# Mixers and projections of a hybrid diffusion step put into the kernel's own list schedule

## The chip, the cores and the metric

The kernel runs on one core of a Trainium2 chip. The metric is the device time of one launch in microseconds (us); the median of three runs of the kernel before is 824.52 us (822.47 to 827.32). Engines are called as the profile calls them: PE (TensorE, matmul) with PEld (its weight loads), DVE (VectorE), ACT (ScalarE), POOL (GpSimd) and SP (SyncE, which issues most DMAs).

## The reference, cut to what matters

One layer over 128 context and 512 latent tokens, model width 1024, everything in float32:

```python
h = rmsnorm(x, norm1_g) * (1 + scale1) + shift1
proj = h @ w_in                      # 1024 -> 3360 columns, split among four head groups
o_a = hgrn2_mixer(...)               # A: gated linear recurrence, two directions, 4 heads of 64
o_b = gla_mixer(...)                 # B: gated linear attention, two directions, 4 heads of 32
o_c = rglru_mixer(...)               # C: convolution, gates, elementwise recurrence (RG-LRU)
o_d = short_conv_mixer(...)          # D: short gated convolution
x = x + gate1 * (concatenate([o_a, o_b, o_c, o_d]) @ w_out)
h2 = rmsnorm(x, norm2_g) * (1 + scale2) + shift2
x = x + gate2 * (square(relu(h2 @ mlp_w1)) @ mlp_w2)
y = rmsnorm(x, final_norm_g)         # and the final states of A, B and C for the context
```

The scales, shifts and gates come from two condition vectors through a 1024 x 6144 matrix (`ada_w`).

## The kernel before

All 640 tokens stay on chip, channels on the partitions. Exact products are made of two rounded parts: a weight chunk is loaded raw (`rawX`), its rounded copy is `hiX`, the rest `loX` (`prep`, line 464), and each projection is 48 matmuls of 320 columns (hi x hi, hi x lo, lo x hi over eight blocks of the 1024 rows).

Four stages follow one another. In the start (0 to some 58 us) x is normalised and transposed, the first modulations are made, and the first chunks `a0` and `q` are projected by an order written out by hand (`START`). In the mixers (58 to 325 us) the names of `PLAN` (line 33) are gone through: a projection of one 128-channel half of a chunk (`cx0`), three units for each v projection (`vi0`), one modulation unit (`ada31`), or the next step of a job. There are four jobs, written as Python generators: `A0`, `A1` and `B` are `gla_job` (line 877), `RG` is `rg_job` (line 1083). A GLA job computes its lower-triangular products by doubling block sizes (`LEVELS`, 1 to 128): at each level a copy `K` of the keys (128 x 640), copies `Qb` of the queries (two 64 x 640 for A, eight 32 x 320 for B, whose heads are half as wide), small matmuls `sA` or `sB`, a masked copy of their results into `W`, and two DVE updates of `G` (lines 944, 945), which holds keys and queries and which the next level reads. Then come transposes `kt`, state sums `ds`, outputs `o`, and a norm over each head (`head_norms`, `NA` and `NB`). B takes over buffers of A0 and A1: there are two `G` and two `F` tiles. Projections share two PSUM buffers (`psA`, tag `mm`), weight chunks two hi/lo pairs and one raw buffer (`wpool`). Temporaries come from pools with a fixed number of buffers for each tag.

The order of instructions in the mixers is made by the framework's scheduler, which follows program order where operands are ready. Which engine makes a copy is looked up by name: `cp` (line 458) takes DVE if the name stands in `ON_DVE` (line 42), otherwise ACT. All copies of one level of one job have one name. `lnexp` (line 452) forces one ACT table set for a pair of functions.

From the output projection on (325 to 818 us), operations are not issued at once but recorded by a list planner (`Plan`, from line 146). Its engines record each call with a duration by formula (`cost`), the operations it depends on, and for tiles the regions read and written. `emit` computes for each operation the latest start that delays nothing after it, then goes through time: of the ready operations of the engine that comes free first, the one with the earliest latest start is issued. A DMA is priced at its bytes over one serial link plus 2 us. Tiles (`LateTile`) are placed when their first use is issued; tiles of one tag take their buffers in the order in which they were recorded (`Slots`). The MLP's matmuls keep their recorded order (`plan.chain`). Between mixers and MLP stand the gate row's store to DRAM (`gate_rows`, line 558), the split of the mixers' results (`put_o`, line 869) and the load and split of the output weights (`wo_v`, `wo_x`); before the change these were issued directly, and the pools of the MLP are opened when those of the mixers are closed.

## Time and profile before

| | |
|---|---|
| median of three runs | 824.52 us |
| profiled execution, time / span | 819.71 us / 817.9 us |
| busy PE / DVE / ACT / POOL | 778.8 / 575.2 / 420.3 / 23.4 us |
| busy PE in 58 to 325 us (mixers) | 255.0 of 267 us |
| busy DVE, ACT in 58 to 325 us | 201.3, 155.0 us |
| busy PE in 550 to 800 us (MLP) | 250.0 of 250 us |
| granted clock of PE | 1.00 in every slice to 800 us |

Busy is the union of the times in which an engine has an instruction in work. A matmul's shown time includes its passage through the array, so consecutive matmuls overlap, and PE can be busy throughout while its matmuls start later than they could. A chain of waits follows the end of a stretch back to what released each instruction.

### The profile page before, as it was taken

To read this page: it belongs to the slowest core of one execution; us is meant where nothing else is said; L and a number is where in the kernel's file an instruction comes from. 1 tells how busy PE (TensorE), PEld (TensorE's weight loads), DVE (VectorE), ACT (ScalarE), POOL (GpSimd) and SP (SyncE) were. 2 spreads that over 40 slices of the span, in tenths; PEclk is the share of its full clock that TensorE was granted. 3 is DMA by queue.
4 is the path that set the end of the run, shared out by engine and by line. 5 is a ranking of instruction groups with operands and counts; after the bars stand their busy time and mean duration, and the time that the engine had idled before them with its cause. 6 is when DMAs were issued, how large, how long until landed. Compare 5 with 4: busy or idle time off the path is not lost.

```text
span 817.9 us, 13749 instructions
## 1 busy us (share of the span) xinstructions
PE 778.8 (95%) x5536; PEld 682.7 (83%) x5536; DVE 575.2 (70%) x1061; ACT 420.3 (51%) x708; POOL 23.4 (3%) x48
## 2 busy tenths in 40 slices
PE   4999999999999989999899999899999999999995
PEld 3798988768777889888888989789899898998984
DVE  4779988857786376368997888647466475675757
ACT  7533549688486332156784706417246172371533
POOL 0040000101010000000000000000000000000001
PEclk9999999999999999999999999999999999999998
DMA  9723323333321522543653636513132041330313
GB/s 352 304 83 137 105 95 142 116 110 100 125 84 56 104 103 65 194 155 127 204 165 102 195 97 204 119 40 117 50 131 75 20 136 52 101 106 2 128 52 128
DMA packets 33696, 97.79 MB, mean 120 GB/s; under 512 B 8672, under 2 KB 9696, under 8 KB 29024
## 3 DMA queue, kind: packets, MB, share of 16 engines
q1 hardware_dynamic: 32544, 95.72, 35.5%
q10 hardware_dynamic: 576, 1.00, 0.4%
q8 instruction: 43, 0.70, 0.3%
q0 software_dynamic: 512, 0.20, 0.1%
q14 instruction: 21, 0.17, 0.1%
HBM read 91.44 MB, written 5.46 MB: 118 GB/s over the span
## 4 chain that ended last, share of the span: by engine, by line
PE 63%; DVE 15%; ACT 10%; DMA 8%; issue 3%; SPq 0%; DVEq 0%; ACTq 0%
PE ps L248 45%; DMA wq<-in_w_dram 4%; ACT QbB L462 2%; DVE xl L248 2%; PE pjcx L492 2%; PE pjdb L492 2%; PE pja L666 2%; DMA w2raw<-in_wout_dram 1%; PE ap L536 1%; DVE wq L248 1%; DMA w2raw<-in_w_dram 1%; PE pjbqk L492 1%; DVE big L248 1%; PE rg L1132 1%; DMA rawdb<-in_win_dram 1%
## 5 line engine op out<-in xcount | busy, mean ns | idle before, releaser
L248 PE MATMUL ps<-vh,olo 128*128 128x512 f32 x680 | 186.4, 390 | 1.0 <-DVE olo L248 0.7
L248 PEld LDWEIGHTS ps<-vh,olo 128*128 128x128 f32 x680 | 126.9, 188 | 28.8 <-DVE olo L248 1.9
L248 PE MATMUL ps<-vl,olo 128*128 128x512 f32 x320 | 99.3, 390 | 0.0
L248 ACT ACTIVATE vh<-w2raw 128x1024 fp32r<-128x1024 f32 x32 | 33.8, 1057 | 118.6 <-PE ps L248 114.2
L248 ACT ACTIVATE xh<-wq 128x512 fp32r<-128x512 f32 x96 | 59.4, 628 | 61.1 <-PE ps L248 43.9
L248 PE MATMUL ps<-yh,xh 128*128 128x320 f32 x256 | 79.5, 311 | 1.2 <-DVE rb L248 1.2
L248 PE MATMUL ps<-yl,xh 128*128 128x320 f32 x256 | 79.0, 309 | 0.0
L248 PE MATMUL ps<-yh,xl 128*128 128x320 f32 x256 | 79.0, 308 | 0.0
L248 DVE TENSOR_TENSOR h<-ps,h 128x512 f32<-128x512 f32 x60 | 38.6, 686 | 52.9 <-PE ps L248 52.6
L248 PEld LDWEIGHTS ps<-vl,olo 128*128 128x128 f32 x320 | 60.1, 188 | 12.7
L248 DVE TENSOR_TENSOR xl<-wq,xh 128x512 fp32r<-128x512 f32 x96 | 64.8, 687 | 8.1 <-ACT xh L248 7.9
L248 PE MATMUL ps<-ohi,xh 128*128 128x320 f32 x256 | 57.1, 310 | 0.5 <-ACT xh L248 0.4
L248 ACT ACTIVATE rb<-rb 128x640 f32<-128x640 f32 x64 | 46.8, 734 | 7.6 <-DVE rb L248 6.8
L248 PEld LDWEIGHTS ps<-yh,xh 128*128 128x128 f32 x256 | 48.1, 188 | 2.0 <-DVE rb L248 1.5
L248 PEld LDWEIGHTS ps<-yl,xh 128*128 128x128 f32 x256 | 48.1, 188 | 0.3
L248 PEld LDWEIGHTS ps<-yh,xl 128*128 128x128 f32 x256 | 48.1, 188 | 0.0
L248 DVE TENSOR_TENSOR vl<-w2raw,vh 128x1024 fp32r<-128x1024 f32 x32 | 39.0, 1220 | 8.1 <-ACT vh L248 7.4
L248 PEld LDWEIGHTS ps<-ohi,xh 128*128 128x128 f32 x256 | 42.8, 188 | 1.1 <-ACT xh L248 0.6
L248 PE MATMUL ps<-ohi,xl 128*128 128x320 f32 x128 | 39.8, 311 | 0.5 <-DVE xl L248 0.4
L248 DVE TENSOR_TENSOR olo<-rb,olo 128x640 fp32r<-128x640 f32 x32 | 26.3, 821 | 18.6 <-ACT olo L248 18.6
L248 PE MATMUL ps<-t,xh 128*128 128x320 f32 x128 | 28.7, 311 | 0.7 <-DVE rb L248 0.7
L248 ACT ACTIVATE rb<-ps 128x320 f32<-128x320 f32 x64 | 27.1, 424 | 4.1 <-PE ps L248 4.1
(426 smaller groups left out, 1677.7 us busy)
## 6 DMA issues: line engine op xcount, KB each, us to landing
ar<-in_ada_w_dram SPq DMA_DIRECT2D x20, 1024.0 KB, 4.9
wq<-in_w_dram SPq DMA_DIRECT2D x72, 256.0 KB, 3.7
w2raw<-in_w_dram SPq DMA_DIRECT2D x32, 512.0 KB, 4.4
big<-in_ada_g_dram SPq DMA_DIRECT2D x8, 512.0 KB, 3.5
x<-in_x_dram SPq DMA_DIRECT2D x5, 512.0 KB, 6.8
big<-in_x_dram SPq DMA_DIRECT2D x5, 512.0 KB, 4.2
x1d<-big SPq DMA_DIRECT2D x5, 512.0 KB, 2.6
xa<-x1d SPq DMA_DIRECT2D x5, 512.0 KB, 4.5
```

The source lines that it names most:

```text
L248: return fn(*[r(x) for x in a], **{w: r(v) for w, v in k.items()})
L462: act.activation(out, src, AF.Copy)
L492: pe.matmul(ps[:, n, :320], wt[:, k, c0:c0 + 128], h[:, k, s], start=(k == 0 and wt is hi and h is hhi), stop=stop)
L536: pe.matmul(ps[32 * g:32 * g + 32, :256], scx[:, 4 * j + g, 2 - 2 * vi:34 - 2 * vi], r3[:, 4 * j + g, :], start=(vi == 0 and j == 0), stop ...
L666: pe.matmul(d, w[:, k, 128 * j:128 * j + 128], (hlo if hi_ else hhi)[:, k, c], start=begin, stop=end, skip_group_check=(ch == "q" and i == 1))
L1132: pe.matmul(ps, wrg[:, dl, j, g, :], xc[:, hN * n:hN * n + hN], start=True, stop=True)
```

## The change

The mixers, their projections, the head norms, the split of the results and the output weights' loads are recorded by the same planner as the MLP, in one plan. `either` records a copy for two engines (`flex`): it is ready on both, and the one that takes it first keeps it. The plan is given times at which engines come free (`free`) and at which the first projections land (`ready`), counted from the mixers' start. Pools of the MLP open by events in the plan, after all uses of the pools whose place they take have been issued. A tile's later uses are ordered behind its first, and the latest start of a tile's first use is at most that of the next tile of the same tag. `PLAN` and the buffer counts stay; it now sets the recorded order, and with it the order in which tiles take their buffers.

```diff
--- before.py
+++ after.py
@@ -40,9 +40,7 @@
...
@@ -147,7 +145,8 @@
 
-    def __init__(self, nc, like):
+    def __init__(self, nc, like, ready=(), free=None):
+        self.ready, self.free, self.first, self.flex = dict(ready), dict(free or {}), {}, {}
         self.nc, self.like, self.ops, self.seen, self.masks = nc, like, [], {}, {}
         self.chain, self.last_pe, self.hint, self.tiles_of = False, None, None, {}
@@ -247,7 +246,22 @@
             r = lambda x: x.real() if isinstance(x, Late) else x
             return fn(*[r(x) for x in a], **{w: r(v) for w, v in k.items()})
+        for x in ins:
+            if not isinstance(x, Late):
+                for name, t in self.ready.items():
+                    if x.tensor.name.startswith(name):
+                        self.first[len(self.ops)] = t
         return self.add(eng, dur, go, ins, outs, mb, sets)
+
+    def either(self, act, dve, a):
+
+        i = self.record("DVE", dve, "tensor_copy", a, {})
+        other = self.ops[i][:3]
+        out, src = a
+        self.ops[i][:3] = ["ACT", self.cost("ACT", "activation", out, [src], (out, src, None), {})[0],
+                           lambda: act(*[x.real() if isinstance(x, Late) else x for x in a], AF.Copy)]
+        self.flex[i] = other
+        return i
     def add(self, eng, dur, fn, ins=(), outs=(), mb=0.0, sets=None, after=()):
         i = len(self.ops)
@@ -272,6 +286,8 @@
                     k.slots.queue.append(k)
                     if k.pool.opened is not None:
                         order.add(k.pool.opened)
+                elif k.users[0] != i:
+                    order.add(k.users[0])
                 k.users.append(i)
                 k.pool.users.append(i)
         if eng == "PE":
@@ -301,8 +317,15 @@
             for p, q in zip(x.queue, x.queue[x.n:]):
                 if max(p.users) < q.users[0]:
                     back.setdefault(q.users[0], []).extend(p.users)
+        before = {}
+        for x in slots:
+            for p, q in zip(x.queue, x.queue[1:]):
+                before.setdefault(q.users[0], []).append(p.users[0])
         for i in range(n - 1, -1, -1):
             eng, dur, _, deps, order, mb, _ = ops[i]
+            for d in before.get(i, ()):
+                if d < i:
+                    latest[d] = min(latest[d], latest[i])
             for d in deps:
                 e2, d2 = ops[d][0], ops[d][1]
                 latest[d] = min(latest[d], latest[i] - d2 - tail[d] - (hop[e2] if e2 != eng else 0.0))
@@ -317,7 +340,7 @@
                 after[d].append((i, True))
             for d in o[4]:
                 after[d].append((i, False))
-        at, free, ready, end_of = [0.0] * n, {}, {}, [0.0] * n
+        at, free, ready, end_of = [self.first.get(i, 0.0) for i in range(n)], dict(self.free), {}, [0.0] * n
         starts = {}
         for x in slots:
             for k in x.queue:
@@ -341,6 +364,8 @@
                         at[i] = max(at[i], end_of[j] + (0.03 if same else hop[ops[j][0]]))
                 x.taken += 1
             ready.setdefault(ops[i][0], []).append(i)
+            if i in self.flex:
+                ready.setdefault(self.flex[i][0], []).append(i)
         for i in range(n):
             if not left[i]:
@@ -362,6 +387,10 @@
             else:
                 i = min(xs, key=lambda x: (latest[x], x))
             ready[eng].remove(i)
+            if i in self.flex:
+                ready["ACT" if eng == "DVE" else "DVE"].remove(i)
+                if eng == "DVE":
+                    ops[i][:3] = self.flex[i]
             _, dur, _, deps, _, mb, sets = ops[i]
             load = None
             if sets and held not in sets:
@@ -448,15 +477,18 @@
         dve.reciprocal(rs, sd)
         return rs
+    recording = []
+
     @contextmanager
     def lnexp(after):
-        with tc.issue_after(after.ins):
-            ld = act.preload_act_table_set("natural_log_exp_and_others")
-        with tc.issue_after(ld.ins):
-            yield
+        plan.hint = "natural_log_exp_and_others"
+        yield
+        plan.hint = None
     def cp(name, out, src):
-        if name in ON_DVE:
+        if recording:
+            plan.either(real_nc.scalar.activation, real_nc.vector.tensor_copy, (out, src))
+        elif name in ON_DVE:
             dve.tensor_copy(out, src)
         else:
             act.activation(out, src, AF.Copy)
@@ -707,8 +739,14 @@
         dve.tensor_scalar(oml, lbt, -1.0, 1.0, op0=OP.mult, op1=OP.add)
     me_, ml_ = ExitStack(), ExitStack()
-    me = me_.enter_context(tc.tile_pool(name="mixe", bufs=1, reuse_waits="tile"))
-    mp = ml_.enter_context(tc.tile_pool(name="mixl", bufs=1, side="right", reuse_waits="tile"))
+    plan = Plan(nc, par[:, 0:1].tensor, ready={"pja0": 7.5, "pjq": 18.4}, free={"PE": 18.2, "ACT": 7.5, "DVE": 8.4})
+    me = LatePool(plan, me_.enter_context(tc.tile_pool(name="mixe", bufs=1, reuse_waits="tile")))
+    mp = LatePool(plan, ml_.enter_context(tc.tile_pool(name="mixl", bufs=1, side="right", reuse_waits="tile")))
+    real_nc, const0 = nc, const
+    recording.append(plan)
+    act, dve, pe, pool = plan.engines()
+    nc = Queues(plan, nc)
+    const, wpool, psA = LatePool(plan, const0), LatePool(plan, wpool, bufs=2), LatePool(plan, psA, psum=True, bufs=2)
     def tmp(nm):
         return mp.tile([128, 658], F32, name=nm, tag="tmp", bufs=NTMP)
@@ -717,6 +755,8 @@
         return tmp(nm)[:, :T]
     def sub(t, g, off, ap):
+        if isinstance(t, Late):
+            return t.view(lambda x: sub(x, g, off, ap))
         v = t[:, g, off:off + 1]
         return bass.AP(tensor=v.tensor, offset=v.offset, ap=[list(v.ap[0])] + ap)
@@ -1219,15 +1259,28 @@
         else:
             do_unit(u)
         if u == "q1":
-            psS_stack.close()
-            psB = stB.enter_context(tc.tile_pool(name="psB", bufs=2, space=PS, reuse_waits="tile"))
+            def open_psB():
+                psS_stack.close()
+                psB.real = stB.enter_context(tc.tile_pool(name="psB", bufs=2, space=PS, reuse_waits="tile"))
+
+            psB = LatePool(plan, psum=True, bufs=2)
+            psB.opened = plan.event(open_psB, range(len(plan.ops)))
     grow1 = gate_rows("gt1", nc.sync)
+    on_rows = on_first = list(range(len(plan.ops)))
     for j in jobs.values():
         assert next(j, None) is None
-    me_.close()
-    lp = ctx.enter_context(tc.tile_pool(name="mlp", bufs=1, reuse_waits="tile"))
+    lp, rp, ls, psN = (LatePool(plan) for _ in range(4))
+
+    def open_lp():
+        me_.close()
+        lp.real = ctx.enter_context(tc.tile_pool(name="mlp", bufs=1, reuse_waits="tile"))
+
+    lp.opened = plan.event(open_lp, me.users)
     oT["hi"] = [lp.tile([128, 2, T], F32R, name=f"ohi{i}", tag=f"ohi{i}") for i in range(4)]
     oT["lo"] = [lp.tile([128, T], F32R, name=f"olo{i}", tag=f"olo{i}") for i in range(8)]
+    VH, VL = ([lp.tile([128, D], F32R, name=f"{nm}{i}", tag=f"{nm}{i}") for i in range(4)] for nm in ("vh", "vl"))
+    BIG = [lp.tile([128, D], F32, name=f"big{i}", tag=f"big{i}") for i in range(2)]
+    WRAW2 = [lp.tile([128, D], F32, name=f"w2raw{i}", tag=f"w2raw{i}") for i in range(2)]
     for j in range(2):
         put_o(4 + j, [(slice(0, 128), hs[j][:, 0:128]), (slice(128, T), hs[j][:, 134:646])])
     for j in range(2):
@@ -1236,19 +1289,21 @@
         put_o(2 + j, [(ALL, pb[j]["o"])])
     for j in range(2):
         put_o(6 + j, [(ALL, dd["o", j])])
-    ml_.close()
-    hw_.close()
-    plan = Plan(nc, par[:, 0:1].tensor)
-    rp = LatePool(plan, ctx.enter_context(tc.tile_pool(name="mlpr", bufs=1, side="right", reuse_waits="tile")))
-    ls = LatePool(plan, ctx.enter_context(tc.tile_pool(name="mlps", bufs=1, reuse_waits="tile")))
-    stB.close()
-    psA_.close()
-    psN = LatePool(plan, ctx.enter_context(tc.tile_pool(name="psN", bufs=1, space=PS, reuse_waits="tile")), psum=True)
-    lp = LatePool(plan, lp)
-    VH, VL = ([lp.tile([128, D], F32R, name=f"{nm}{i}", tag=f"{nm}{i}") for i in range(4)] for nm in ("vh", "vl"))
-    BIG = [lp.tile([128, D], F32, name=f"big{i}", tag=f"big{i}") for i in range(2)]
-    WRAW2 = [lp.tile([128, D], F32, name=f"w2raw{i}", tag=f"w2raw{i}") for i in range(2)]
-    act, dve, pe, pool, sync = (Now(e) for e in (act, dve, pe, pool, nc.sync))
+
+    def open_rest():
+        ml_.close()
+        hw_.close()
+        rp.real = ctx.enter_context(tc.tile_pool(name="mlpr", bufs=1, side="right", reuse_waits="tile"))
+        ls.real = ctx.enter_context(tc.tile_pool(name="mlps", bufs=1, reuse_waits="tile"))
+
+    def open_psum():
+        stB.close()
+        psA_.close()
+        psN.real = ctx.enter_context(tc.tile_pool(name="psN", bufs=1, space=PS, reuse_waits="tile"))
+
+    rp.opened = ls.opened = plan.event(open_rest, [lp.opened] + wpool.users + mp.users + on_rows)
+    psN.psum = True
+    psN.opened = plan.event(open_psum, psA.users + psB.users + on_first)
     HT = T // 2
     HALVES = (slice(0, 512), slice(512, 1024))
...
...
```

## Rows read from the trace of the kernel before

**Rows 1.** The page, busy us (share of the span) xinstructions.

```profile
PE 778.8 (95%) x5536; PEld 682.7 (83%) x5536; DVE 575.2 (70%) x1061; ACT 420.3 (51%) x708; POOL 23.4 (3%) x48
```

**Rows 2.** Sums by stretch: length, busy PE, PEld, DVE, ACT, POOL, clock, DMA, GB/s.

```profile
58.00:325.00 267.00, 255.01 (x2588) 218.50 (x2587) 201.29 (x388) 154.98 (x248) 10.95 (x22) 1.00 0.31 101
58.00:110.00 52.00, 50.96 (x665) 48.23 (x664) 50.68 (x106) 20.41 (x29) 0.00 (x0) 1.00 0.30 106
200.00:270.00 70.00, 63.58 (x625) 52.25 (x626) 50.19 (x104) 46.54 (x85) 2.57 (x6) 1.00 0.24 80
270.00:325.00 55.00, 52.23 (x350) 49.70 (x351) 32.16 (x46) 15.45 (x21) 0.22 (x4) 1.00 0.33 84
325.00:550.00 225.00, 219.23 (x1149) 190.81 (x1149) 168.12 (x335) 114.09 (x204) 0.00 (x0) 1.00 0.47 146
550.00:800.00 250.00, 250.00 (x1398) 227.51 (x1397) 157.13 (x237) 112.50 (x187) 0.00 (x0) 1.00 0.26 83
```

**Rows 3.** Groups of PE's instructions, 58 to 325 us: count, busy us, mean ns, idle before.

```profile
L492 PE MATMUL pjcx<-hhi,hicx 128*128 128x320 f32 x32 | 7.4, 312 | 0.0
L536 PE MATMUL ap<-ar,scx 128*32 128x256 f32 x192 | 13.6, 383 | 0.5 <-ACT o2a L1073 0.5
L962 PE MATMUL sB<-QbB,KB 128*32 128x128 f32 x280 | 12.4, 277 | 3.6 <-ACT QbB L462 3.1 <-DVE QbB L460 0.5
L962 PE MATMUL sA<-QbA,KA 128*32 128x64 f32 x560 | 10.5, 221 | 0.8 <-DVE QbA L460 0.8
L1132 PE MATMUL rg<-xc,wrg 128*128 128x323 f32 x32 | 12.0, 471 | 0.7 <-ACT gr L1143 0.6
```

**Rows 4.** Chain of waits, 90 to 120 and 140 to 200 us: start, length, what.

```profile
92.45 1.25 PE sA L962 x80
...
103.82 7.06 PE pjcx L492 x48
...
114.70 1.31 PE sA L989 x20
...
144.04 1.00 PE ap L536 x16
...
154.69 0.89 PE dsA L1023 x8
...
163.28 1.28 PE rg L1132 x4
...
178.73 0.85 PE sB L962 x20
```

**Rows 5.** Chain of waits, 198 to 246 us, its shares by engine and line.

```profile
by line: ACT QbB L462 35.2%; DVE QbB L460 9.9%; ACT TB L462 7.7%; DVE GB L944 6.7%; DVE GB L945 6.2%; issue 5.7%; DVE WB L971 3.5%; ACT TB L993 3.4%; ACT KB L462 3.1%; ACT gelu L802 2.9%; ACT L802 2.7%; ACT TB L994 2.5%; PE sB L962 1.8%; DV
```

**Rows 6.** Timeline of ACT, three levels of job B: start, length, instruction, count.

```profile
195.22 5.08 ACT L462 ACTIVATE QbB<-GB 32x320 f32<-32x320 f32 x8
...
203.58 4.22 ACT L462 ACTIVATE QbB<-GB 32x320 f32<-32x320 f32 x8
...
215.59 3.92 ACT L462 ACTIVATE QbB<-GB 32x320 f32<-32x320 f32 x8 [0.22 <-DVE GB L945]
```

**Rows 7.** Groups of DVE's copies: QbB in 58 to 325, QbA in 58 to 110 us.

```profile
L460 DVE COPY QbB<-GB 32x320 f32<-32x320 f32 x16 | 5.1, 317 | 0.2
...
L460 DVE COPY QbA<-GA 64x640 f32<-64x640 f32 x8 | 3.9, 485 | 0.1
```

**Rows 8.** Timeline of ACT, 281 to 290 us; in brackets idle before, and releaser.

```profile
284.57 2.23 ACT L130 ACTIVATE vh<-w2raw 128x1024 fp32r<-128x1024 f32 x2 [8.74 <-DMA w2raw<-in_wout_dram]
...
288.51 0.68 ACT L812 ACTIVATE sgb<-pjbg 128x640 f32<-128x640 f32 x1
```

**Rows 9.** DMA issues, 255 to 300 us: count, KB each, median us to landing.

```profile
rowgt<-gt SPq DMA_DIRECT2D x2, 4.0 KB, 10.8
```

**Rows 10.** Groups of ACT's instructions, 58 to 325 us, a table load.

```profile
L802 ACT ACT_TABLE_LOAD x1 | 1.3, 1283 | 0.0
```

**Rows 11.** Timeline of PE, 281 to 326 us, the first matmul of a projection.

```profile
291.81 0.53 PE L492 MATMUL pjdv<-hhi,hidv 128*128 128x320 f32 x2 [0.47 <-DVE sgb L813]
```

More of the change, by code (lines that the diff above doesn't have):

```diff
@@ L42 @@
 ON_DVE = """
-DA000 DA010 DA030 DA120 DB01 DB10 DB20 DB31 KA02 KA032 KA04 KA08 KA164 KA18 KB16 KB32 KB64 KB8 QbA016 QbA032 QbA04
-QbA064 QbA164 QbA18 QbB1 QbB32 QbB8 TA010 TA030 TA120 TA130 TB01 TB11 TB21 TB30 dc0 dc1 hi_a1 hi_ag hi_bg hi_bqk hi_cg
-hi_db hi_i hi_o3 kTA01 kTA11 kTB0 oA10 oB0 oB1 oT0 oT3 oT6 oT7 q0 vi1 vi2 xT2 xT4
+xT2 xT4
 """.split()
@@ L1290, in wo_x @@
                 raw = WQ[2 * k + n]
-                sync.dma_start(raw, A["wout"][i][:, D * k + 512 * n:D * k + 512 * n + 512])
+                nc.sync.dma_start(raw, A["wout"][i][:, D * k + 512 * n:D * k + 512 * n + 512])
                 split(XH[j], XL[j], raw)
@@ L1296, in wo_v @@
             j = k0 + k
-            sync.dma_start(WRAW2[k], A["wout"][i][:, D * k:D * k + D])
+            nc.sync.dma_start(WRAW2[k], A["wout"][i][:, D * k:D * k + D])
             split(VH[j], VL[j], WRAW2[k])
@@ L1304, in hybrid_step_kernel @@
     wo_x(3, 4)
-    act, dve, pe, pool = plan.engines()
-    nc = Queues(plan, nc)
     last_used = [2, 0, 3, 1]
```

## The prediction, made before the result was known

> **What bounds the kernel now.** I read the page's table of busy time first: TensorE (PE) is busy in 95% of the span [rows 1]. A change of order cannot shorten PE's work, so only the time in which PE does nothing, or less than it could, is to be had. The sums by stretch say where that is [rows 2]. From 550 to 800 us, in the MLP whose order the list planner already makes, PE is busy in 250.00 of 250 us. From 325 to 550 us it misses 5.8 us. In the mixers and projections, 58 to 325 us, which is what the change touches, it misses 12.0 of 267 us, and 6.4 of those lie in the 70 us from 200 to 270.
>
> Busy time flatters PE, because a matmul's shown end overlaps the start of the next. So I set PE's work in 58 to 325 us against the fastest pace that the trace shows for each kind: records by kind [rows 3] times the time of one record where they stand back to back [rows 4].
> - The projections' 320-column records: 27 groups like the pjcx row, 32 records each, so 864. At 7.06 / 48 = 0.147 us that is 127.1 us.
> - ap: 192 at 1.00 / 16 = 0.0625 us, 12.0 us. sB: 280 at 0.85 / 20 = 0.0425, 11.9 us. sA: 560 at 1.25 / 80 = 0.0156, 8.8 us. rg: 32 at 1.28 / 4 = 0.32, 10.2 us.
> - The other 2588 - 1928 = 660 at the pace of dsA, 0.89 / 8 = 0.111 us: 73.3 us. About 160 of them fill half the height; at 1.31 / 20 = 0.066 us they would take 7 us less.
>
> That makes 243 us, or 236: PE could be through 24 to 31 us sooner. I use 27. It is the ceiling of what reordering can give here; half of it hides inside "busy".
>
> What holds PE up is told by the chain of waits from 198 to 246 us [rows 5]: hardly any PE in it. It is the second GLA job, B, going through its eight levels on VectorE (DVE) and ScalarE (ACT): 35% copies QbB on ACT, 10% the same on DVE, plus work foreign to the job (gelu and its table load, 2.9% and 2.7%). The rows of ACT show why: eight QbB copies of one level stand one behind the other for 5.08, 4.22 and 3.92 us [rows 6], because the hand-written list names an engine for all copies of a level at once. Early on the picture is another: from 58 to 110 us DVE is busy 50.68 of 52 us and ACT 20.41 [rows 2]. There the first job, A0, waits for DVE, and B can't start before A0 and A1 give back the buffers it shares with them (two of each for three jobs).
>
> **The change, part by part.**
>
> *Copies go to whichever engine is free.* In B's levels, a QbB copy takes 0.53 us on ACT (4.22 / 8) and 0.317 on DVE [rows 6, 7]. Eight of them, five on DVE and three on ACT, take 1.6 us. Against a mean of 4.2 for the four levels now on ACT that is 2.6 each, 10.4 us; against 8 x 0.317 = 2.5 for two later levels on DVE it is 0.9 each, 1.8 us. Together 12 us, if both engines had nothing else; they are busy in 72% and 66% of 200 to 270 us [rows 2], so I take three quarters: 9 us. The bounds are 0 (the second engine never free at that moment) and 12. In the early stretch DVE carries 11.2 us of copies in seven groups, the largest 3.9 us [rows 7]. If half of them go to ACT, which idles in 60% of that stretch, the DVE-bound stage shortens by 5.6 us; bounds 0 and 11.
>
> *Order by lateness instead of by program order.* Work foreign to B's chain moves off it: gelu and its table load are 5.6% of 48 us, 2.7 us; I take 3 with what else is in it. No instruction is removed, and PE's instructions stay what they are.
>
> *The boundary to the MLP.* From 270 to 325 us PE misses 2.8 us [rows 2]. The cause is a queue: the gate row's store, 4 KB in small pieces, takes 10.8 us to land [rows 9]; the output weights behind it on SP's queue land late; ACT sits 8.74 us at their split, and behind that wait are the split of a projection's weights and a gate's epilogue [rows 8]. The planner can now move all of these, but it prices this store as 2 us. Bounds: 2.8 us gained, or the whole 10.8 lost if PE has no projection left as filler at that moment. I take 1.5 gained. New order edges (output weights of the left pool before the last mixer buffer is given back, the whole right pool and its loads after all of them) repeat what the pools' closing did before: nothing.
>
> *Release times and waits at the start.* The planner is told when PE, ACT and DVE come free and when the first projections land. It is not told that the first two weight chunks still hold both weight buffers, so it may queue the split of the third ahead of other work, and that engine waits until PE gives the buffer back. Behind it stand the first sigmoid, which waits for the same matmuls, and small RG-LRU work; 0 to 3 us on an engine, nothing on PE, which has the q projection to do until 58 us. I take 0.
>
> *Table loads on ACT.* There are 21 in 58 to 325 us, in eight rows like the one shown, 1.28 us each, 27 us [rows 10]. The planner may group them or, in mixing jobs, add some; ten more would be 13 us on an engine idle for 112 of 267 us. I count 0. The Trainium skill (ScalarE: Activation LUTs, Table sets: the hidden batching unit; What ACT_TABLE_LOAD costs) tells authors to finish all work of one set before switching and puts a switch at about 2.7 us, drain included, which speaks against interleaving jobs; the row shows 1.28 and no added drain. By the page's price, ten more would be an estimated 27 us of ACT time, still less than its idle time, so the sum would stay.
>
> Sum: 9 + 3 + 5.6 + 1.5 = 19 us, under PE's ceiling of 27. What is late next is PE itself: some 8 us of slack would remain, 3% of the stretch, as much as the planner leaves in 325 to 550 us (5.8 of 225). The profiled execution took 819.7 us, 4.8 under the median of 824.5; 19 less makes it 800.7, and with those 4.8 a median of about **805 us**.
>
> **The rivals.**
> - *PE becomes the bound almost everywhere*: all of the 27 us, and 2 to 3 of the 5.8 us that 325 to 550 misses. About 795 us. For it: the same planner leaves nothing idle after 550 us. Against it: there, long operands are ready far ahead, while the mixers are chains of half-microsecond steps, and each error in a planned duration stalls an in-order engine.
> - *The gain is given back at the boundary*: the slow store takes 10.8 us of DMA while the mixers have run out of filler, and the split copies block ACT and DVE. 805 + 10.8 to 805 + 16: 816 to 821 us. For it: the planner's price of the store. Against it: in the kernel before, only 2.8 us came of it.
> - *Slower: projections jam.* The projections use two PSUM buffers in strict order. If lateness puts their epilogues behind B's chain, both buffers stay held, and PE loses its filler. Projections are 127 of 267 us, so the 70 us of B's levels hold 33 us of them; all of it pushed behind the chain costs 33 against a gain of 19: 838 us. It decides from 19 us of held-up filler. For it: the case is in the trace, a gate's epilogue that PE's next projection waits for [rows 11]. Against it: that wait is 0.47 us, and the planner passes the lateness of the next user on to the epilogue.
> - *The copies don't move*: if the greedy choice gives ACT the same copies, only 3 + 1.5 us remain, about 820 us.
>
> **How the numbers follow.** Forecast 805 (797 to 813): 0.54. PE-bound, near 795: 0.18. Given back or copies not moved, 814 to 824: 0.14, half of it over the bound of 0.5%, about what a measurement of this kernel can tell from no change. Jammed, above 828: 0.14. So faster 0.77, same 0.09, slower 0.14. The range from 788 (the 27 us, the 5.8 us of 325 to 550 and a fast run) to 828 leaves out the jam and little else.
>
> **What would show it.** QbB copies of one level on both engines at once; B's last level nearer 220 than 240 us; DVE under 90% and ACT over 50% from 58 to 110 us; the first matmul of the output projection near 306 instead of 325 us, and everything after it shifted without change. Wrong if the table loads rise by more than 20, if PE waits for projections' epilogues, or if PE's idle time in the mixers stays at 12 us.

## The result, and the profile after

The changed kernel takes 833.39 us (median of four runs, 830.22 to 835.23); the kernel before takes 823.5 us in the same comparison (822.24 to 827.32). The ratio is 1.0108 with a 95% interval of 1.0061 to 1.0156: slower by about 1%. The forecast was 805 us, faster; size and sign are both wrong, and the range (788 to 828) doesn't hold the time.

The page of the changed kernel, busy time of each engine and PE's granted clock in 40 slices of the span of 831.2 us (answers to [rows 1]):

```profile
PE 789.8 (95%) x5536; PEld 687.3 (83%) x5536; DVE 568.7 (68%) x1053; ACT 430.0 (52%) x715; POOL 23.6 (3%) x48
...
PEclk9998999999999999999999999999999999999999
```

The same 5536 matmuls keep PE busy for 11.0 us more than before, and the share stays 95%: the loss doesn't look like waiting. One slice, the fourth, has an 8 in the clock. The sums by stretch (columns as in [rows 2]; the fourth and fifth rows are new cuts):

```profile
58.00:110.00 52.00, 47.41 (x646) 42.87 (x644) 36.09 (x80) 29.52 (x40) 0.00 (x0) 0.93 0.23 84
200.00:270.00 70.00, 64.21 (x634) 50.02 (x635) 57.60 (x120) 48.84 (x83) 5.28 (x7) 1.00 0.30 105
270.00:325.00 55.00, 55.00 (x390) 51.53 (x387) 24.31 (x38) 21.75 (x29) 0.21 (x4) 1.00 0.39 97
325.00:337.00 12.00, 12.00 (x76) 11.13 (x75) 5.74 (x11) 4.10 (x7) 0.21 (x4) 1.00 0.00 0
550.00:800.00 250.00, 250.00 (x1399) 227.49 (x1398) 154.84 (x231) 110.55 (x182) 0.00 (x0) 1.00 0.26 83
69.60:76.40 6.80, 6.15 (x32) 4.97 (x33) 0.00 (x0) 0.00 (x0) 0.00 (x0) 0.50 0.42 154
```

The first matmul of the output projection starts at 337.3 us, before at 325.0; from it to the end there are 493.9 us, before 492.9. So 12.3 of the 13.3 us between the two profiled spans arise in the mixers. PE's own waiting hardly rose: the kernel before misses 12.0 of 267 us in its mixers [rows 2], the new one about 13 of 279.

Two things stand out. The first is at 70 us. PE's timeline (start, length, instruction, count, in brackets idle before and releaser):

```profile
66.86 0.60 PE L247 MATMUL pja<-hhi,loa 128*128 128x320 f32 x3
70.25 1.94 PE L247 MATMUL ap<-ar,scx 128*32 128x256 f32 x16 [2.79 <-DMA ar<-in_ada_w_dram]
...
74.69 1.27 PE L247 MATMUL pja<-hhi,loa 128*128 128x320 f32 x4
...
78.98 0.75 PE L247 MATMUL pja<-hhi,loa 128*128 128x320 f32 x4
...
80.54 0.74 PE L247 MATMUL sA<-QbA,KA 128*32 128x64 f32 x40
```

PE waits 2.79 us for a modulation's weights, and behind that wait the granted clock is 0.50 (1.2 GHz) from 69.6 to 76.4 us: the 16 ap take 1.94 us in place of 1.00 [rows 4], four pja 1.27 in place of 0.75. The Trainium skill (TensorE: Matmul & The Clock Gate, Part 1: The HAM clock gate) calls the halved clock the default from which activity releases PE; by that rule a stall costs more than its own length, and the trace agrees. ACT's timeline of the same run:

```profile
50.63 0.63 ACT L262 ACTIVATE hia<-rawa 128x512 fp32r<-128x512 f32 x1 [2.88 <-PE pja L698]
...
62.51 3.02 ACT L262 ACTIVATE QbA<-qA 64x640 f32<-64x640 f32 x4 [1.21 <-DVE qA L247]
...
79.62 0.70 ACT L247 ACTIVATE FA<-pja 128x640 f32<-128x640 f32 x1 [12.79 <-PE pja L247]
```

The plan put the split of the third weight chunk (`hia`) where its buffer was still in use by PE; ACT stood still for 2.88 us, and the raw buffer and the loads behind it came later than planned. They did not come later than in the kernel before. SP issues the modulation's loads at 65.46 us here, at 67.69 in the kernel before, and at 65.32 in e1 (below), where the stall is gone (SP's timelines, in this order):

```profile
65.46 7.10 SPq L247 DMA_DIRECT2D ar<-in_ada_w_dram  x2
67.69 7.60 SPq L1177 DMA_DIRECT2D ar<-in_ada_w_dram  x2
65.32 6.41 SPq L247 DMA_DIRECT2D ar<-in_ada_w_dram  x2
```

What differs is PE's order. The changed kernel places the 16 `ap` behind 155 of the 192 `pja` records and ahead of every `sA`; the kernel before has them behind all 192 and behind two groups of `sA` (its PE timeline):

```profile
65.35 0.77 PE L962 MATMUL sA<-QbA,KA 128*32 128x64 f32 x40
...
73.86 1.05 PE L536 MATMUL ap<-ar,scx 128*32 128x256 f32 x16
```

The first `sA` of the changed kernel starts at 80.5 us, although the four `QbA` copies were done at 65.5 (ACT's second row). ACT and DVE then lack work for some 13 us, because the order by lateness lets the first job's small matmuls stand back (in recorded order, e9 below, the first `sA` starts at 65.0), and the stall adds to it.

The second thing is in the chain of waits from 200 to 265 us, with B's levels at 217 (start, length, what):

```profile
217.71 0.34 PE sB L247 x4
218.06 0.34 PE pjag L247
218.40 0.35 PE sB L247 x6
218.75 0.34 PE pjag L247
219.09 0.35 PE sB L247 x6
219.44 0.34 PE pjag L247
```

Before, 20 sB stood in one block of 0.85 us [rows 4] behind waits for copies [rows 5]. Now the copies are spread over both engines, each releases a few sB, and the planner, for which these are due soonest, puts one projection matmul between every two handfuls. At the pace of [rows 4] a pair of lines (six sB, one 320-column record) is 6 x 0.0425 + 0.147 = 0.40 us; it takes 0.69. PE is never idle there and still loses 0.29 us with each change to and fro between the rounded projections and the plain small matmuls. B's levels as a whole are shorter than before, 68.3 us from the first `sB` to the last (194.7 to 263.0) against 73.9 (169.1 to 243.0). They start 25.6 us later, since A's last `sA` starts at 183.7 us, before at 142.5.

Over the whole of the mixers I compared each PE record's start-to-start time with its kind's back-to-back pace. The medians say that a change from projection to small matmul costs 92 ns and one back 134, so 0.23 us a round trip, in both kernels. Along the order of the records there are 61 round trips before and 85 after: 24 x 0.23 = 5.4 us. With the 1.1 us by which PE's waiting rose in all and 3.4 us lost at half clock (half of the 6.8) that is 9.9 of the 12.3 us. This is bookkeeping; the runs below test it.

### The profile page after: what moved, and what is told of

It reads as the page before. It is cut to its first block, busy times and chain, and to the rows that moved or that the text cites. A ratio compares the mean times of both kernels' runs of the same rounds, so it can differ in the third digit from the quotient of the medians.

```text
span 831.2 us, 13785 instructions
## 1 busy us (share of the span) xinstructions
PE 789.8 (95%) x5536; PEld 687.3 (83%) x5536; DVE 568.7 (68%) x1053; ACT 430.0 (52%) x715; POOL 23.6 (3%) x48
## 4 chain that ended last, share of the span: by engine, by line
PE 76%; DVE 11%; ACT 5%; DMA 4%; issue 3%; SPq 0%; DVEq 0%; ACTq 0%
PE ps L247 48%; DMA wq<-in_w_dram 3%; PE pjag L247 2%; PE pjdv L247 2%; PE pjdc L247 2%; PE pja L698 2%; PE vbv L247 2%; PE pjbg L247 2%; PE ap L247 2%; PE pjdb L247 2%; PE sB L247 2%; PE pjcg L247 1%; DVE xl L247 1%; PE pjbqk L247 1%; DVE GA L247 1%
## 5 line engine op out<-in xcount | busy, mean ns | idle before, releaser
L247 ACT ACTIVATE vh<-w2raw 128x1024 fp32r<-128x1024 f32 x36 | 38.0, 1057 | 121.3 <-PE ps L247 113.9
L247 ACT ACTIVATE xh<-wq 128x512 fp32r<-128x512 f32 x104 | 64.6, 628 | 68.4 <-PE ps L247 42.8
L247 DVE TENSOR_TENSOR xl<-wq,xh 128x512 fp32r<-128x512 f32 x104 | 70.2, 688 | 16.5 <-ACT xh L247 16.2
L247 DVE TENSOR_TENSOR vl<-w2raw,vh 128x1024 fp32r<-128x1024 f32 x36 | 43.8, 1221 | 8.4 <-ACT vh L247 7.8
```

Of the source, the lines that this page charges most:

```text
L247: return fn(*[r(x) for x in a], **{w: r(v) for w, v in k.items()})
```

## The experiments

Medians in us; the ratio is to the kernel before in the same comparison.

| run | median | ratio (95%) | round trips |
|---|---|---|---|
| changed kernel | 833.39 | 1.0108 (1.0061 to 1.0156) | 85 |
| e1_release | 837.87 | 1.0226 (1.0198 to 1.0253) | 87 |
| e2_list_engines | 837.27 | 1.0211 (1.0172 to 1.0251) | 94 |
| e3_both | 837.66 | 1.0209 (1.0189 to 1.0228) | 91 |
| e4_split_qbb | 820.52 | 0.9995 (0.9975 to 1.0015) | 56 |
| e5_recorded_order | 832.10 | 1.0119 (1.0047 to 1.0191) | 59 |
| e6_switch_price | 845.40 | 1.0269 (1.0214 to 1.0325) | 58 |
| e7_store_last | 819.10 | 0.9973 (0.9931 to 1.0015) | 61 |
| e8_split_store | 814.71 | 0.9898 (0.9846 to 0.9949) | 56 |
| e9_order_store | 821.93 | 0.9979 (0.9951 to 1.0007) | 59 |
| e10_release_store | 831.49 | 1.0103 (1.0054 to 1.0152) | 87 |
| e11_after_store | 834.26 | 1.0142 (1.0087 to 1.0196) | 85 |
| e12_order_list_store | 835.16 | 1.0124 (1.0059 to 1.0189) | 57 |
| e13_late_half | 827.98 | 1.0095 (1.0061 to 1.0129) | 85 |
| e14_early_half | 826.05 | 1.0059 (1.0033 to 1.0085) | 64 |
| e15_order_costs | 822.94 | 1.0022 (0.9990 to 1.0054) | 58 |

**The early stall and the engines' choice.** e1 tells the plan when the third chunk's buffer comes free; e2 gives each copy the engine of the old list; e3 does both.

```diff
+        for x in outs:                                     # e1, in record()
+            if isinstance(x, Late) and x.tile.args[2] == "hia1":
+                self.first[len(self.ops)] = 10.4
-    plan = Plan(..., ready={"pja0": 7.5, ...
+    plan = Plan(..., ready={"pja0": 10.4, ...
-        if recording:                                      # e2, in cp()
-            plan.either(...)
-        elif name in ON_DVE:
+        if name in ON_DVE:
```

> The changed kernel with two release times put right: the split of the third weight chunk and the first sigmoid may not start before 10.4 us of the plan, when PE gives the first weight buffer back. Theory of the early slip (PE waits 2.8 us for a modulation chunk at 67.5 us, its clock falls to half until 76 us, ACT and DVE idle 12 us, and job B starts 11 us later): that wait goes, the clock stays at 1.00, B starts 8 to 10 us earlier, 822 to 826 us. Rival, the plan is too optimistic everywhere and the early stall is only one of many: the stall goes, but the time falls by 3 to 4 us alone, 829 to 830.

> The changed kernel, but each copy on the engine that the old hand list gives it; order by lateness and all else as in the changed kernel. Theory that the free choice is right and the order at fault: slower than the changed kernel by 4 to 9 us, 837 to 842. Rival, the greedy choice is at fault (copies put on ACT where DVE would have been done sooner): 820 to 828.

> Release times put right and the hand list's engines. If both faults are small and independent, the sum of the two effects of e1 and e2 against the changed kernel, some 829 to 834. If the list is the better choice, under 822, below the kernel before.

In e1 the stall at 70 us is gone, and the kernel is not faster but, by the intervals, slower than the changed one. The plan now has the `ap` behind 171 of the `pja` records in place of 155, so PE waits 0.17 us for the weights. The `sA` still stand back (e1's timeline of PE):

```profile
70.28 1.07 PE L247 MATMUL ap<-ar,scx 128*32 128x256 f32 x16 [0.17 <-DMA ar<-in_ada_w_dram]
...
74.56 0.77 PE L247 MATMUL sA<-QbA,KA 128*32 128x64 f32 x40
```

What e1 won at the start it lost in B's levels, where PE waits 3.8 us for `QbB` copies on ACT, and near the end of the mixers. e1's timeline of PE there, the first matmul of the last projection:

```profile
314.57 0.90 PE L247 MATMUL pjdb<-hhi,hidb 128*128 128x320 f32 x2 [5.78 <-ACT hidb L265]
```

what ACT did for it:

```profile
312.61 1.91 ACT L265 ACTIVATE hidb<-rawdb 128x2048 fp32r<-128x2048 f32 x1 [12.41 <-DMA rawdb<-in_win_dram]
```

and its DMA issues, 255 to 345 us (KB each, median us to landing):

```profile
rawdb<-in_win_dram SPq DMA_DIRECT2D x1, 1024.0 KB, 12.0
rowgt<-gt SPq DMA_DIRECT2D x2, 4.0 KB, 13.1
```

The last chunk's load and the gate's two row stores run at the same time, and the load needs 12.0 us where it took 5.1 in e4 and e5, which issue it well after the stores. Two loads of `w2raw` run beside it too; in e10 (below), which has these without the stores, it takes 6.0. The early stall alone doesn't explain the loss. Nor does the free choice of engine: without it the kernel is no faster (e2, e3), and e3 misses the 829 to 834 that was expected if the two faults were independent.

**The boundary's stores.** e4 is the kernel *before* with only the copies of B shared, five to DVE and three to ACT at each level: the prediction's largest term alone. e7 is the kernel before with the two row stores moved behind the last chunk's load on SP; e8 has both.

```diff
+                        eng = "xT2" if 4 * i + g < 5 else "QbB"        # e4, e8: on the list or not
-                            cp(f"Qb{jn}{b}", qd, ...)
+                            cp(eng, qd, ...)
-    grow1 = gate_rows("gt1", nc.sync)
+    with tc.issue_after(loads["db"].ins): grow1 = gate_rows("gt1", nc.sync)   # e7, e8
```

> The kernel before, with one part of the change done by hand: of the eight QbB copies of each level, five on DVE and three on ACT. By the prediction's term this is worth 9 us (0 to 12): 812 to 815 us. Rival, PE has other work to fill with while B's chain runs, or the two engines are busy with other work at those moments: 820 to 824, no change.

> The kernel before with its two 4 KB row stores of the gate moved on SP's queue from ahead of the four w2raw loads to behind the last chunk's load. In the kernel before PE is busy through 270 to 325 and waits 0.5 us there, so if PE's own work sets the boundary, nothing moves: 821 us, within 1. If the stores' 10.8 us do hold back the loads that the boundary needs, up to 2 us are gained: 819.

> The kernel before with both: the second mixer's Qb copies of a level shared five to VectorE and three to ScalarE, and the two row stores moved behind the last chunk's load. Theory 'given back at the boundary': the split alone ended the second mixer 4.4 us sooner and lost it in a wait of 6.0 us of PE for the gate's epilogue (the first output-projection matmul at 325.4), whose engines were held by splits that waited for w2raw, and these loads were behind the row stores; with the stores last the wait shrinks and about 4 us stay: 816 to 817, first output-projection matmul near 321. Rival 'bound by PE's own work': the time stays at 820 to 821.

In e4, B's levels are through 4.4 us sooner (the state sums `dsB` behind them start at 241.3 against 245.7) and the time doesn't move. e4's timeline of PE at the boundary, to be set beside [rows 11]:

```profile
293.12 0.87 PE L492 MATMUL pjdv<-hhi,hidv 128*128 128x320 f32 x2 [6.03 <-DVE sgb L813]
```

and of ACT, beside [rows 8]:

```profile
287.06 1.06 ACT L130 ACTIVATE vh<-w2raw 128x1024 fp32r<-128x1024 f32 x1 [4.04 <-DMA w2raw<-in_wout_dram]
289.82 0.68 ACT L812 ACTIVATE sgb<-pjbg 128x640 f32<-128x640 f32 x1
```

The 0.47 us of [rows 11] have become 6.03: the gate's activation `sgb` stands on ACT behind a split that waits for `w2raw`, and that load is behind the row stores. In e8, with the stores last, the same lines of ACT come 8 us sooner:

```profile
279.09 1.06 ACT L130 ACTIVATE vh<-w2raw 128x1024 fp32r<-128x1024 f32 x1 [3.88 <-DMA w2raw<-in_wout_dram]
281.86 0.68 ACT L812 ACTIVATE sgb<-pjbg 128x640 f32<-128x640 f32 x1
```

because w2raw lands in 4.2 us, against 7.9 in e4, and the four loads take turns in two buffers, so that the difference counts twice (e8's DMA issues, 255 to 345 us):

```profile
w2raw<-in_wout_dram SPq DMA_DIRECT2D x4, 512.0 KB, 4.2
```

e8 takes 814.71 us, 1.0% under the kernel before: faster than both kernels, with two small edits. The moved store by itself (e7) is worth 0.3%, with an interval that holds no change; the split copies by themselves nothing; together they give 8.9 us, about what the prediction's copies were to give; that the numbers meet is luck, since that term has no store in it.

**Recorded order and late stores in the plan.** e5 is the changed kernel with, for the mixers, recorded order (that of `PLAN`) as the priority in place of lateness. e9 is e5 with the row stores behind the last w2raw and the last chunk; e10 is e1 with these late stores, e11 the changed kernel with them and nothing else.

```diff
+        for i in range(self.mixers):                                  # e5, e9, in emit()
+            latest[i] = 0.01 * (i - self.mixers) - 1000.0
-    grow1 = gate_rows("gt1", nc.sync)                                 # e9, e10, e11
...
     wo_v(0, 2)
+    grow1 = gate_rows("gt1", nc.sync)
+    for i in (1, 2):
+        plan.ops[-i][4].update(loads[x] for x in ("db", "w2"))
```

> The changed kernel with one thing different: among the mixers' and projections' operations that could start, the planner takes the one recorded first (the order that the unit plan of the kernel before gives) in place of the one due soonest; copies still go to whichever engine is free, release times and all else stay. Theory 'order': the lateness key itself is what loses, because it jumps between the accumulating projections and the small mixer matmuls whenever a due time says so (85 round trips between the two kinds before the first output-projection matmul, against 61 in the kernel before; in this order there are 59 planned). At the 0.23 us that one round trip costs in the trace, 26 fewer are 6 us: the first output-projection matmul near 331 in place of 337 and a time of about 827, and about 823 if the stall at 70 us goes as well. Rival 'fixed plan': any order that is fixed ahead from the planner's optimistic durations loses the same, because what slips on the chip is not re-ordered: 832 to 838, with the same lack of busy PE in the mixers as the changed kernel.

> The changed kernel with the mixers' operations taken in recorded order, and the two 4 KB row stores of the gate put behind the last w2raw load and the last chunk's load on SP's queue. In the run with the recorded order alone, PE kept pace with the kernel before up to about 245 us (second mixer's last level 249 against 243) and then waited 10.5 us for the gate's epilogue, with the clock at half for some time behind it. Theory 'two losses': the order by lateness costs the start and the stores cost the boundary, each enough by itself to use up the gain; with both mended the wait goes and the time is 819 to 822, first output-projection matmul near 326. Rival 'fixed plan': another wait takes its place, as before, and it stays at 830 or more.

> The changed kernel with the corrected release times of the third weight chunk (no stall at 70 us) and the row stores put behind the last w2raw and last chunk loads; the order is still that by lateness. The run with the release times alone lost, late in the mixers, 5.8 us of PE waiting for the last chunk and some 3 us at half clock behind it, and 3.8 us on the second mixer's copies. Theory 'two losses': the boundary's part goes, and with it about 8 us: 829 to 831, which is a little under the changed kernel and still slower than before by the rest (more changes of kind, the copies that are late). If it falls to 823 or less, the order by lateness costs nothing by itself; if it stays at 836 or more, the stores are not the cause of that wait.

> The changed kernel with nothing but the row stores put behind the last w2raw and last chunk loads. In the changed kernel PE was busy through 270 to 325, so the stores held back nothing there that was due: 832 to 834, no change. A time under 829 would say that the stores cost the changed kernel something that its waits don't show.

e5 has no stall at 70 us and PE is busy throughout 58 to 110 us, yet the time is that of the changed kernel. Most of what it won goes at the boundary. PE's wait in e5's timeline:

```profile
304.51 0.87 PE L247 MATMUL pjdv<-hhi,hidv 128*128 128x320 f32 x2 [10.53 <-DVE sgb L247]
```

and the sums by stretch around it (columns as in [rows 2]):

```profile
294.00:304.40 10.40, 0.00 (x0) 0.00 (x0) 4.19 (x4) 4.58 (x5) 0.00 (x0) 0.75 0.57 56
304.50:311.30 6.80, 6.79 (x31) 6.80 (x32) 1.58 (x2) 2.53 (x2) 0.00 (x0) 0.63 0.42 157
```

PE does nothing for 10.4 us, and the clock is at 0.63 on the mean of the next 6.8. e9 removes just that: 821.93 us, the same as the kernel before within its interval. Its sums for 58 to 110, 200 to 270 and 270 to 325 us:

```profile
58.00:110.00 52.00, 52.00 (x715) 48.98 (x717) 47.06 (x96) 28.63 (x41) 0.00 (x0) 1.00 0.26 91
200.00:270.00 70.00, 64.67 (x654) 54.52 (x652) 55.52 (x123) 44.59 (x80) 4.63 (x11) 0.98 0.22 78
270.00:325.00 55.00, 53.53 (x360) 51.26 (x359) 30.34 (x45) 18.16 (x24) 0.22 (x4) 1.00 0.31 96
```

e10 stands at a ratio of 1.0103 where e1 stood at 1.0226, so the stores cost e1 some 10 us; its 831.49 us is at the edge of what the theory of two losses expected. e11 shows that the stores cost the changed kernel itself nothing, since its projections come so late that PE has filler throughout 270 to 325 us. So three costs hide one another: with the start and the stores mended, order by lateness is still 9.6 us over recorded order (e10 against e9). e9 has not e1's release times; e11 and e9 differ in the order alone, and there lateness costs 12.3 us.

**What the order by lateness costs.** e6 prices each change of kind at 0.11 us in the plan and holds a matmul of the other kind back by 3 us. e13 takes recorded order for all recorded before B's first step and lateness for the rest, e14 the reverse; both have e10's release times and late stores.

```diff
+                i = min(xs, key=lambda x: (latest[x] + (3.0 if kind[x] != last_kind else 0.0), x))   # e6, PE
+        for i in range(self.half):                                                     # e13
+            latest[i] = 0.01 * (i - self.half) - 1000.0
+        for i in range(self.half):                                                     # e14
+            latest[i] -= 2000.0
+        for i in range(self.half, self.mixers):
+            latest[i] = 0.01 * (i - self.mixers) - 1000.0
```

> The changed kernel with one thing different: when the planner takes the next matmul, one of the other kind than the last (rounded projections against plain 4-byte small matmuls) counts as due 3 us later, and each change of kind is planned with 0.11 us. All durations, releases and the free choice of engine for copies stay. The plan then has 58 round trips between the kinds in place of 85. Theory 'round trips': 27 x 0.23 = 6 us less, about 827 us, first output-projection matmul near 331. Theory 'order' (the lateness key loses because it drains the second mixer's chain too late, whatever the kinds): no gain or a loss from delaying urgent small matmuls, 833 or more.

> Release times and late row stores as in the run that has both with the order by lateness; but all that is recorded before the second mixer's first step goes first and in recorded order, and only what is recorded from there on is ordered by lateness. The plan has 85 round trips between the kinds of matmul, as many as with lateness throughout. Theory 'second half': the 9 us arise where the second mixer's chain, the gate's and the last projections compete, since there lateness alternates kinds and lets the chain's end slip (last level at 298.8 against 247.1): 829 to 831. Rival 'first half' (the first mixer's order, which leaves VectorE idle early on): 822 to 824.

> The opposite: what is recorded before the second mixer's first step goes first, ordered by lateness, and the rest in recorded order; release times and late row stores stay. The plan has 64 round trips. Theory 'second half': 822 to 824, within 2 us of the recorded order throughout. Rival 'first half': 829 to 831. If both halves cost, both runs lie near 826.

e6 has the 58 round trips that were planned and is the slowest of all. Two things are mixed in it. Its first output-projection matmul comes at 338.9 us, 1.6 later than in the changed kernel, so in the mixers the 27 round trips saved (6 us by the medians) were used up by waits, of which the third below is the changed kernel's stall, and by the clock, 0.93 from 200 to 270 us against 1.00 (PE's waits in e6, 40 to 345 us: total, times, longest):

```profile
PE sB L250 <- issue: 3.4, 1, 3.4
PE rg L250 <- DVE StA L250: 3.1, 2, 2.5
PE ap L250 <- DMA ar<-in_ada_w_dram: 2.8, 1, 2.8
PE sB L250 <- DVE WB L250: 2.1, 1, 2.1
```

The other 9 us are lost behind the mixers, where the penalty acts too, which I had not meant: PE waits 10.2 us for the norm's rows `rb` there, 3.6 in the changed kernel. So few round trips are not enough, and a penalty is no remedy.

In the records, e10's excess over back-to-back pace is 47.3 us and e9's 38.3. The 9.0 us between them stand beside the 9.6 measured; they are the same time counted another way, and only their split says more. About 4 are the hidden cost of 28 more round trips (excess at the changes of kind, visible gaps taken off: 11.0 against 7.0 us). PE's waiting is the same, some 12 us in both. In B's stage the clock is 0.93, against 0.98 in e9; e10's sum:

```profile
200.00:270.00 70.00, 63.78 (x615) 53.55 (x604) 57.94 (x125) 40.74 (x73) 5.45 (x11) 0.93 0.26 92
```

From these two rows I estimate 0.05 x 70 = 3.5 us lost by the clock; some 1.5 us stay open. The price of a round trip has thus been counted, not varied by itself: e6, which was to vary it, changed other things too.

e13 and e14 are both slower than e9 beyond their intervals, so each half by lateness costs something. e13 can't be told from e10, and e14's interval overlaps e10's, so the shares are not settled.

**The free choice in recorded order, and the planned durations.** e12 is e9 with the old list of engines; e15 is e9 with the planner's durations raised to what the trace shows.

```diff
-        if recording:                                                  # e12: as e2
-            plan.either(...)
-            return 0.16 + n / 1900, 0.0                                # e15, tensor_copy on DVE
+            return 0.27 + n / 1900, 0.0
+            extra = 0.1 if op == "activation" and a[2] is None else 0.0   # e15, copy on ACT
```

> As the run with recorded order and late stores, but each copy stays on the engine that the hand-written list of the kernel before gives it, so the two runs differ in the free choice of engine alone. In the kernel before, sharing the second mixer's Qb copies between both engines ended its last level 4.4 us sooner, and with the stores out of the way the kernel took 1.0% less. Theory 'free choice is worth something': this run is 3 to 6 us slower than the one with free choice, 823 to 827. Rival 'no worth' (the free choice puts copies where the planner's too short durations say, and the list did as well): within 2 us of it.

> Recorded order and late row stores, and the planner's durations raised to what the trace shows: a copy on VectorE by 0.11 us, on ScalarE by 0.10, the states' small additions to 0.4 us, the second mixer's 32-row matmuls by 45%. If the choice of engines suffers from the short durations (PE waits 5.2 us for Qb copies on ScalarE in the run without this), the second mixer's last level comes 3 to 5 us sooner, 243 instead of 247, and the time is 817 to 819. Rival: the plan's durations change nothing that the chip doesn't even out: 821 to 823.

e12 is 13 us slower than e9; 3 to 6 were expected. With the list, ACT and DVE wait for each other in B, and PE for weight splits on DVE. From e12's waits, 160 to 340 us (total, times, longest):

```profile
DVE GB L249 <- ACT QbB L249: 9.2, 4, 4.7
...
ACT QbB L249 <- DVE GB L249: 7.3, 2, 4.8
```

The list was made for the framework's order, so this is the worth of the choice in the plan's order, not of the choice as such.

Set beside e7, e12 shows something else. Both have the old list of engines and the stores behind the loads (e12's also behind the last w2raw); they differ in who makes the order of the mixers and the boundary. e12 stands at 1.0124 (1.0059 to 1.0189), e7 at 0.9973 (0.9931 to 1.0015): some 12 us. From the first `sB` to the last, B's levels take 96.6 us in e12 (168.4 to 265.0), 74.0 in e7 (169.6 to 243.6) and 75.9 in e9 (170.9 to 246.8). So the planner's order costs this much even without lateness, and the free choice only earns it back. No run here separates why. e15 took away PE's wait for Qb copies on ACT (5.2 us in e9) and got 4.1 us for the split `lobg` in its place; the time is e9's. As far as these raised durations go, it is not the short durations that kept the change from gaining.

## Why the prediction was wrong, point by point

- **The step that failed: order by lateness, +3 us, "PE's instructions stay what they are".** They do, but their sequence does not. Lateness costs 9.6 us against recorded order (e10, e9; 12.3 in e11 and e9), which is a term mis-sized by 13 us with the wrong sign. The records that I used for the ceiling of 27 us had both kinds in blocks [rows 4]; I read the excess over that pace as slack for a better order to fill, and part of it is the price of alternating, which a finer order raises: by the count of each kind's pace the excess went from 39.0 us before to 51.0 after.
- **A cost put at nothing: the planner's order itself.** Against its "PE-bound" rival the prediction says that each error in a planned duration stalls an in-order engine, but its sum has no term for it. With the old engines the planner's recorded order is some 12 us slower than the framework's (e12, e7). The free choice of engine is worth 13 us in that order (e9, e12), near the 9 + 5.6 forecast for the copies in the other order, and is spent on it: e9 takes what the kernel before takes. Why the order costs this stays open; e15 speaks against the durations that it raised.
- **Copies on both engines, 9 us.** The mechanism was right and the size about double what came: B's levels were through 4.4 us sooner in e4, not 9. That this gain reaches the end was the error: it was late by 6.0 us at the boundary, the next thing in line. With the stores moved the pair is worth 8.9 us (e8 against before). In the changed kernel the copies do move (25 of the 320-column QbB copies from `G` on DVE, 23 on ACT), and B's levels are 5.6 us shorter, but they start 25.6 us late.
- **The early, DVE-bound stretch, 5.6 us.** Right where the order lets it be: in e9, DVE is busy 47.06 of 52 us (50.68 before [rows 2]), ACT 28.63 (20.41), and A's last `sA` ends at 137.4 us against 142.8. By the end of B's levels it is gone (`dsB` from 248.6 against 245.7). In the changed kernel DVE is under 90% and ACT over 50%, as I said a success would look, in a stretch where both stood still for some 13 us: those marks could not tell a shorter stage from a stalled one.
- **The release times, "nothing on PE".** I named the mechanism (the third chunk's split queued while both weight buffers are held) and bounded it at 3 us on an engine. I did not follow it into PE's planned order: the plan took the modulation's weights to land sooner than they could and put the `ap` too early, so PE waited 2.79 us and ran 6.8 us at half clock. Mended alone (e1) it shows no gain; with the late stores it is 2.8 us (e10 against e11), within the intervals.
- **The boundary, +1.5 us, bounds -10.8 to +2.8.** 0 in the changed kernel (e11). The lower bound was real in others: 10.5 us of waiting in e5, and 10 us between e5 and e9. The rival "given back at the boundary" is thus shown in e1, e4 and e5, but not as the cause in the changed kernel.
- **Table loads, 0.** Right: 20 of 1.28 us in the mixers, 21 before [rows 10].
- **The rivals.** "Jammed" gave a time near the result (838) by a mechanism that isn't there: from 270 to 337 us PE is busy throughout and waits for nothing. "PE-bound" holds in a sense that I did not mean: PE is busy, and some 5 of the 12.3 us are its own alternation. My own sign of failure, idle time staying at 12 us, came true, and would have missed most of the loss, which is in busy time.

## What to carry to other kernels

A list scheduler that looks at due times alone can cut the long runs of one kind of matmul into crumbs (61 round trips became 85 here), and a table of busy time shows nothing of it: compare start-to-start time with the back-to-back pace of each kind. Before trusting a gain on one chain, ask what is late next by a few microseconds; here three costs (a stall at the start, two 4 KB stores, the order) each covered the others, so that mending one showed nothing or a loss. Two small edits in the old order (shared copies, the stores moved behind the loads) gave 1.0%, which the new order in none of its forms here did.

## What the runs showed of the hardware that was not expected

- **Half clock behind short waits.** PE's waits of 2.79 us (changed kernel), 5.78 (e1), 6.03 (e4) and 10.53 (e5) were each followed by a stretch at a lower granted clock: 0.50 over 6.8 us in the changed kernel, 0.63 on the mean from 314.6 to 321.0 us in e1, 0.50 from 293.2 to 297.0 in e4, 0.63 on the mean of the 6.8 us that follow in e5. Not every wait was: behind 2.02 us at 252.7 us of the changed kernel the clock stayed at 1.00, and behind the same wait of 1.42 us at 300 us it stayed at 1.00 in the kernel before and was 0.72 on the mean from 300 to 306 us in e7.
- **Alternating kinds of matmul** cost 92 ns into the plain small ones and 134 ns back (medians, the same in both kernels), with PE shown busy.
- **Two stores of 4 KB in 4-byte pieces** (the first gate's) take 10.1 to 15.7 us to land in these runs and can slow what runs beside them. rawdb takes 12.0 us in e1, with the stores and two w2raw loads beside it, and 6.0 in e10, with the w2raw loads alone; w2raw takes 11.1 in e5, behind the stores, and 4.7 in e9. With the stores right behind it rawdb takes 7.5 to 8.9 in e9 and e8 but 5.0 in e14, and 7.6 in the kernel before, where no store is near; so how much they cost a load depends on more than their being there. The Trainium skill (DMA: Bandwidth & Descriptors, Bandwidth) calls transfers under 64 KB dominated by descriptors and gives in its table 0.68 us of engine time for a load of 4 KB, without the issue; the direction agrees, and the price for pieces this small is that of the trace.
